# A two-layer streaming encoder step: order of the mixer's front, the bank of its first projection, and the engine of the norms' sums

## The chip, the cores and the metric

The kernel runs on one core of a Trainium2 chip. The metric is the device time of one execution in microseconds. A core has a matrix engine (TensorE, PE), a vector engine (VectorE, DVE), a scalar engine (ScalarE, ACT), GpSimd (POOL) and queues for DMA (SyncE issues nearly all of them). Each engine works through its own list of instructions in order, and waits on semaphores for the others. The matrix engine writes to PSUM, which has eight banks here; DVE and ACT read it.

## The reference

384 rows (256 prompt frames, 8 × 16 sample frames) of width 1024 pass through two layers. Each layer is

```python
x += 0.5 * rmsnorm(swiglu(rmsnorm(x)))        # ffn1
n  = rmsnorm(x); h = n @ w_in                 # mixer: one projection, split into groups
# query latent (384) | kv latent (256) | rope key (32) | conv 2x256 | gMLP 2x256 | short conv 3x256 | gates 4x1024
y  = sum_b sigmoid(gate_b) * (branch_b @ w_br_b);  x += rmsnorm(y @ w_o)
x += 0.5 * rmsnorm(swiglu(rmsnorm(x)))        # ffn2

def rmsnorm(x, g):
    return x * rsqrt(mean(x * x, -1) + EPS) * g
```

The four branches are an attention over compressed latents (the query and kv latents are each normalised, then expanded), a depthwise convolution of width 31, a gMLP with a layer norm of its right half, and a short convolution. The outputs are x and the new caches (normalised kv latents, rotated rope keys, convolution states, gMLP rows).

## The kernel before

All matrix products are made of three matmuls: each fp32 operand is split into a high part (`wh`, `xh`: copied by ACT to a rounded type) and a low part (`wl`, `xl`: the difference, by DVE), and high × high, high × low and low × high are added in PSUM. The 384 rows are three tiles of 128 (t = 0, 1, 2; t = 2 is the sample). Weights arrive by DMA in a stage (`st`), and become `wh` and `wl` shortly before use; their order is a list of units (`plan_units`, `plan_mixer`, line 565).

**Banks.** Six banks of PSUM are accumulators, `acc(t, h)`; two are used in turn as `rot`. A new tile in a bank waits for all readers of the one before it.

**Order.** The program is written by a planner. The main line of the code emits matmuls one after the other; every matmul moves an assumed clock on (`tick`). Short chains of work, such as a norm with its transposes, are generators that are spawned beside it: each `yield` names the engine that must be done first, and the chain goes on when the assumed time of that engine (costs in `COST`, line 51, and a latency) has come, in the midst of the matmuls of the main line. So costs decide between which matmuls a transpose stands; the order is then fixed on each engine, and only semaphores count on the chip.

**A passage between two stages** (`tails`, `heads`, `chain`, lines 371 to 450). The last stage's sums stand in the accumulators. For each t: ACT squares both halves with a row sum (`junk<-acc`), DVE adds the two sums and EPS in one `tensor_scalar` (`factor`), POOL raises that to the power −0.5 (`power`, tiles `post`), DVE scales and adds to x. Then the same for the next stage's norm (`pre`): square, DVE sum, POOL power, DVE product (`half`). `flip(h)` transposes each half of the normalised tile into `acc(t, h)` by four matmuls with `ident`; ACT copies the result to `xh`, and `low` lets DVE compute `xl` from the same bank. `heads` runs the next stage's first projection for t = 0, 1, 2, each of 24 matmuls (8 blocks of `xh` by `wh` and `wl`, then 8 of `xl` by `wh`).

**The mixer's front** (in layer 0 about 290 to 350 us, in layer 1 about 1210 to 1270 us). In `heads` the first projection (`main`, 416 columns: query latent and rope key, in a `rot` bank) is followed by `latent_q(t)`: ACT squares it (tile `cq`), DVE computes the rope key from it in four operations (`kr`), DVE, POOL and DVE make the norm, and its transposes go to `acc(t, 0)`. Then follow in the main line: the first half of the convolution's inputs, `conv(0)` (two projections of 24 matmuls each, in `rot`); the second projection (`mB`, 512 columns in `acc(t, 1)`), with the chains `latent_kv(t)` (tile `kv`, transposes of `half`, for t = 2 of `lat_s`) and `gmlp_v(t)` (tile `sv`); the queries (`uq`: three small projections with `rotate(t)`, whose results are transposed again, and four with `nope(j)`, which fill `qTp`); then `conv(1)`, keys, values and attention. The remaining dense work (`dense`, line 837) is put between the steps of the attention.

Of the kernel before, what the change touches and what calls it, by code (L numbers as in the profile page):

```python
# [50 lines left out]
COST = {ACT: (95, 0.83), DVE: (65, 1.04), POOL: (150, 2.1)}  # L51
# [10 lines left out]
class Engine:  # L62
# [5 lines left out]
    def __getattr__(self, op):  # L68
# [4 lines left out]
        def call(*args, **kw):  # L73
# [7 lines left out]
            else:  # L81
# [4 lines left out]
                if self.name == DVE and op == "tensor_scalar":  # L86
                    per *= 0.6
                self.core.spend(self.name, fix * (2 if "accum_out" in kw else 1) + per * n)
# [11 lines left out]
class Core:  # L100
# [224 lines left out]
    def power(self, r, v):  # L325
        self.nc.gpsimd.tensor_tensor(r, v, self.neghalf, op=ALU.pow)
# [70 lines left out]
    def chain(self, t, post, stats, gain, at=None):  # L397
# [164 lines left out]
    def plan_mixer(self, units, l):  # L562
# [7 lines left out]
        fm(range(0, 2))  # L570
        for h in range(4):
            units.append((("mB", l, h), a["in_b"][l, :, 2 * h:2 * h + 2, :], [2, 512], "M"))
        for h in range(3):
            units.append((("uq", l, h), a["w_uq"][l, h], [3, 256], "M"))
# [71 lines left out]
    def mixer_front(self, l, m, mf, ma, aT, yT):  # L646
# [201 lines left out]
        with pool("mixq") as mq:  # L848
# [11 lines left out]
            def main(t):  # L860
                pas[t] = self.rot([416])
                return pas[t], lambda k: [w[:, k % 2, :] for w in self.weights(keys[k // 2])]

            def mid(t):
                self.spawn(("cq",), latent_q(t), "rot")

            def latent_q(t):
# [4 lines left out]
                s, v, r = self.rms_stats(pa[:, :QL], "cq")  # L872
# [15 lines left out]
                self.drop("rot")  # L888
# [11 lines left out]

            def latent_kv(t, pb):
                tt = slice(t * P, (t + 1) * P)
                yield PE

                s, v, r = self.rms_stats(pb[:, :KL], "kv")
                yield ACT
                nc.vector.tensor_scalar(v, s, 1.0 / KL, EPS, op0=ALU.mult, op1=ALU.add)
                yield DVE
                self.power(r, v)
                yield POOL  # L910
                lat = lat_s if t == 2 else self.half()[:, :KL]
                nc.vector.scalar_tensor_tensor(lat, pb[:, :KL], r, g_kv, op0=ALU.mult, op1=ALU.mult)
                nc.sync.dma_start(out=a["o_lat"][l, tt, :], in_=lat)
                self.drop("acc")
                yield DVE
                tp = self.acc(t, 0)
                for j in range(2):
                    nc.tensor.transpose(tp[:, j * P:(j + 1) * P], lat[:, j * P:(j + 1) * P], self.ident)
                yield PE
                t2 = tp[:, :KL].rearrange("p (a b) -> p a b", a=2)  # L920
                if t < 2:
                    yield from self.split_into(lth[:, :, tt], ltl[:, :, tt], t2)
                else:
                    nc.scalar.copy(latTs, t2)

            def gmlp_v(t, pb):

                yield PE
                sv = self.small.tile([P, 10], F32, tag="sv", name="sv")
                nc.vector.bn_stats(sv[:, 0:6], pb[:, KL:])  # L930
                nc.vector.bn_aggr(sv[:, 6:8], sv[:, 0:6])
                v, r = sv[:, 8:9], sv[:, 9:10]
                nc.vector.tensor_scalar(v, sv[:, 7:8], EPS, None, op0=ALU.add)
                nc.vector.scalar_tensor_tensor(vn[t], pb[:, KL:], sv[:, 6:7], vn_g, op0=ALU.subtract, op1=ALU.mult)
                yield DVE
                self.power(r, v)
                yield POOL
                nc.vector.scalar_tensor_tensor(vn[t], vn[t], r, vn_b, op0=ALU.mult, op1=ALU.add)
                if t == 2:
                    nc.sync.dma_start(out=a["o_vc"][l], in_=vn[t])  # L940

            for t in range(NT):
                tt = slice(t * P, (t + 1) * P)
                pb = self.acc(t, 1)
                for k in range(KD):
                    w = self.weights(("mB", l, k // 2))
                    self.mm3(pb, (self.xh[:, k, tt], self.xl[:, k, tt]),
                             (w[0][:, k % 2, :], w[1][:, k % 2, :]), k == 0, k == KD - 1)
                    if t == NT - 1 and k % 2:
                        self.done(("mB", l, k // 2))  # L950
                self.spawn(("lat",), latent_kv(t, pb), "acc")
# [584 lines left out]
```

## Time and profile before

| | |
|---|---|
| median of 3 runs | 1859.82 us (1858.51 to 1859.93) |
| profiled execution | 1858.79 us, its span 1857.0 us |
| PE busy | 1831.8 us, 99 % |
| DVE busy | 952.6 us, 51 % |
| ACT busy | 699.7 us, 38 % |
| POOL busy | 47.7 us, 3 % |
| chain that ended last | PE 93 %, DVE 4 %, ACT 1 %, issue 1 % |

Every instruction is issued through one wrapper (line 74), so groups are told apart by their tiles, not by lines. A matmul's busy time overlaps that of the next one; the time from start to start is what it costs in a row of its like.

### The profile page before, as it was taken

Reading aid. Unit: us, or ns where it says so; the run is one execution under the profiler, and the core shown is the slowest. Engines: PE = TensorE matmul, PEld = TensorE weight load, DVE = VectorE, ACT = ScalarE, POOL = GpSimd, SP = SyncE. Lnnn points to the kernel's source line nnn. Section 1 sums busy time; section 2 is a strip of 40 time slices with the busy share of each in tenths; the row PEclk is TensorE's granted clock in tenths of the full one; section 3 lists DMA queues with packets and bytes.
Section 4 is the critical chain, followed back from the end, with each engine's and each line's share of the span. In section 5 each row is a group of like instructions: output and inputs, shape, how many; then the busy total and the mean of one; then the engine's idle time right before and its main releaser. Section 6 shows DMA issues by size and latency. Waiting matters only on the chain.

```text
span 1857.0 us, 25073 instructions
## 1 busy us (share of the span) xinstructions
PE 1831.8 (99%) x10060; PEld 1704.4 (92%) x10060; DVE 952.6 (51%) x1466; ACT 699.7 (38%) x1156; POOL 47.7 (3%) x96
## 2 busy tenths in 40 slices
PE   8999999999999999999999999999999999999998
PEld 6999998889999889999989999988899998999997
DVE  5333347896544463333463333478864446533333
ACT  5333334444333443333343333445343335333332
POOL 0000001000000000000000000010000000000000
PEclk9999999999999999999999999999999999999999
DMA  7444443452343443344444434344523434443441
GB/s 252 137 125 125 125 146 94 142 178 83 114 137 124 146 159 125 125 126 126 134 137 126 128 130 129 117 102 139 173 73 127 142 123 136 148 127 126 133 125 46
DMA packets 98087, 241.88 MB, mean 130 GB/s; under 512 B 28977, under 2 KB 39985, under 8 KB 97970
## 3 DMA queue, kind: packets, MB, share of 16 engines
q1 hardware_dynamic: 97826, 240.21, 41.4%
q8 instruction: 79, 1.29, 0.3%
q14 instruction: 38, 0.31, 0.1%
q10 hardware_dynamic: 144, 0.07, 0.0%
HBM read 236.63 MB, written 3.31 MB: 129 GB/s over the span
## 4 chain that ended last, share of the span: by engine, by line
PE 93%; DVE 4%; ACT 1%; issue 1%; POOL 0%; DMA 0%; POOLq 0%; DVEq 0%; ACTq 0%
PE rot L74 59%; PE acc L74 34%; DVE yTb L74 1%; DVE wl L74 1%; DVE half L74 1%; ACT wh L74 0%; ACT junk L74 0%; DVE sv L74 0%; DVE yTd L74 0%; DVE qTp L74 0%; DVE qa L74 0%; DVE xl L74 0%; DMA st<-in_f 0%; POOL ln L74 0%; POOL kv L74 0%
## 5 line engine op out<-in xcount | busy, mean ns | idle before, releaser
L74 DVE TENSOR_TENSOR wl<-st,wh 128x1024 fp32r<-128x1024 f32 (+3 forms) x426 | 500.1, 1185 | 479.3 <-ACT wh L74 468.3
L74 ACT CAST wh<-st 128x1024 fp32r<-128x1024 f32 (+3 forms) x426 | 428.5, 1018 | 665.1 <-issue 366.3
L74 PE MATMUL rot<-xh,wh 128*128 128x384 f32 x1984 | 669.1, 337 | 0.7 <-ACT sg L74 0.7
L74 PE MATMUL rot<-xh,wl 128*128 128x384 f32 x1984 | 665.7, 336 | 0.6 <-DVE wl L74 0.6
L74 PE MATMUL rot<-xl,wh 128*128 128x384 f32 x1984 | 665.1, 335 | 0.0
L74 PEld LDWEIGHTS rot<-xh,wh 128*128 128x128 f32 x1984 | 372.5, 188 | 8.0 <-issue 3.2
L74 PEld LDWEIGHTS rot<-xh,wl 128*128 128x128 f32 x1984 | 372.6, 188 | 5.0 <-DVE wl L74 1.0
L74 PEld LDWEIGHTS rot<-xl,wh 128*128 128x128 f32 x1984 | 372.5, 188 | 0.3 <-issue 0.3
L74 PE MATMUL acc<-wl,hh 128*128 128x512 f32 x528 | 207.2, 392 | 0.0
L74 PE MATMUL acc<-wh,hl 128*128 128x512 f32 x528 | 207.1, 392 | 0.0
L74 PE MATMUL acc<-wh,hh 128*128 128x512 f32 x528 | 205.4, 389 | 0.0
L74 DVE TENSOR_TENSOR hf<-sg,rot 128x384 f32<-128x384 f32 x80 | 44.4, 555 | 146.0 <-PE rot L74 146.0
L74 PEld LDWEIGHTS acc<-wl,hh 128*128 128x128 f32 x528 | 99.1, 188 | 20.8
L74 PEld LDWEIGHTS acc<-wh,hl 128*128 128x128 f32 x528 | 99.1, 188 | 19.1
L74 PEld LDWEIGHTS acc<-wh,hh 128*128 128x128 f32 x528 | 99.2, 188 | 18.9
L74 ACT ACTIVATE half<-rot 128x384 f32<-128x384 f32 x58 | 28.5, 492 | 167.2 <-PE rot L74 167.2
L74 DVE SCALAR_TENSOR_TENSOR half<-half,acc 128x384 f32<-128x384 f32 x44 | 24.4, 554 | 124.1 <-PE acc L74 124.1
L74 DVE SCALAR_TENSOR_TENSOR yTb<-bs,cols,yTb 128x384 f32<-128x384 f32 x120 | 73.8, 615 | 2.1
L74 PE MATMUL rot<-wl,xh 128*128 128x512 f32 (+1 forms) x144 | 55.7, 387 | 1.6 <-DVE wl L74 1.6
L74 PE MATMUL rot<-wh,xh 128*128 128x512 f32 (+1 forms) x144 | 56.3, 391 | 0.0
L74 PE MATMUL acc<-ident,half 128*128 128x128 f32 x262 | 43.9, 283 | 6.7 <-DVE half L74 5.4
L74 POOL TENSOR_TENSOR post<-post,neghalf 128x1 f32<-128x1 f32 x18 | 12.2, 679 | 1440.2 <-DVE post L74 1440.0
(221 smaller groups left out, 1631.7 us busy)
## 6 DMA issues: line engine op xcount, KB each, us to landing
st<-ffn_gp SPq DMA_DIRECT2D x160, 512.0 KB, 3.5
st<-ffn_dn SPq DMA_DIRECT2D x88, 512.0 KB, 3.5
st<-in_g SPq DMA_DIRECT2D x64, 512.0 KB, 3.7
st<-in_f SPq DMA_DIRECT2D x24, 512.0 KB, 4.0
st<-ffn_gs SPq DMA_DIRECT2D x16, 512.0 KB, 4.8
st<-w_o SPq DMA_DIRECT2D x16, 512.0 KB, 4.2
st<-w_br SPq DMA_DIRECT2D x16, 384.0 KB, 3.1
st<-in_b SPq DMA_DIRECT2D x8, 512.0 KB, 4.9
```

What stands on the lines that cost most here:

```text
L74: r = f(*args, **kw)
```

## The change

Four things are altered.

1. The first projection of the mixer goes to `acc(t, 1)` instead of a `rot` bank, and `latent_q` is a holder of an `acc` bank.
2. The queries (`uq`, with `rotate` and `nope`) stand directly behind `conv(0)`, ahead of the second projection `mB`. The order of the weights is changed with them. `latent_kv` and `gmlp_v` are moved behind them, too.
3. In `dense` the two `mix` steps follow each other, ahead of the two `short_gate` steps.
4. The sums of all norms go from DVE to POOL: one `tensor_tensor` add of EPS (for norms of two halves: EPS to the first sum early, `early`, and the second sum later), then the power. The scale 1/n of the latents' norms is folded in the Square. The planner's cost for POOL is 270 ns plus 2.1 per element instead of 150, and 330 per element for a power.

```diff
-COST = {ACT: (95, 0.83), DVE: (65, 1.04), POOL: (150, 2.1)}
+COST = {ACT: (95, 0.83), DVE: (65, 1.04), POOL: (270, 2.1)}
...
+                if self.name == POOL and kw.get("op") == ALU.pow:
+                    fix, per = 270, 330
...
-    def power(self, r, v):
+    def power(self, r, v, more):
+
+        self.nc.gpsimd.tensor_tensor(v, v, more, op=ALU.add)
         self.nc.gpsimd.tensor_tensor(r, v, self.neghalf, op=ALU.pow)
...
             squared = self.ready(ACT)
+            post.early(stats)
...
             nc.scalar.activation(self.junk(512), x[:, half(h)], AF.Square, scale=1.0 / 32, accum_out=(s0, s1)[h])
+            if h == 0:
+                yield ACT
+                nc.gpsimd.tensor_tensor(v, s0, self.eps, op=ALU.add)
         yield ACT
-        nc.vector.tensor_scalar(v, s0, s1, EPS, op0=ALU.add, op1=ALU.add)
-        yield DVE
-        self.power(r, v)
+        self.power(r, v, s1)
...
-            for f, c in ((short, 0), (short, 1), (mix, 0), (short_gate, 0), (mix, 1), (short_gate, 1), (mix_gate, 0), (mix_gate, 1),
+            for f, c in ((short, 0), (short, 1), (mix, 0), (mix, 1), (short_gate, 0), (short_gate, 1), (mix_gate, 0), (mix_gate, 1),
...
             def main(t):
-                pas[t] = self.rot([416])
+                pas[t] = self.acc(t, 1)[:, :416]
...
-                self.spawn(("cq",), latent_q(t), "rot")
+                self.spawn(("cq",), latent_q(t), "acc")
...
-                s, v, r = self.rms_stats(pa[:, :QL], "cq")
+                s, r = self.rms_stats(pa[:, :QL], "cq")
...
                 yield ACT
-                nc.vector.tensor_scalar(v, s, 1.0 / QL, EPS, op0=ALU.mult, op1=ALU.add)
-                yield DVE
-                self.power(r, v)
+                self.power(r, s, self.eps)
...
-                self.drop("rot")
+                self.drop("acc")
...
-        st = self.stat(tag, 3)
-        self.nc.scalar.activation(self.junk(elements(x)), x, AF.Square, accum_out=st[0])
+        st = self.stat(tag, 2)
+        self.nc.scalar.activation(self.junk(elements(x)), x, AF.Square, scale=elements(x) ** -0.5, accum_out=st[0])
...
+    def early(self, stats):
+        self.nc.gpsimd.tensor_tensor(stats[2], stats[0], self.core.eps4, op=ALU.add)
+
     def factor(self, stats):
         s0, s1, v, r = stats
-        self.nc.vector.tensor_scalar(v, s0, s1, EPS * self.f, op0=ALU.add, op1=ALU.add)
-        yield DVE
-        self.core.power(r, v)
+        self.core.power(r, v, s1)
```

On PE, in layer 0 at the end of the first projection of t = 0 and the start of that of t = 1, the program before had (`acc<-ident,half` are transposes of x's tile t = 1, the projection is the one with 416 columns):

```order
1462 L74 MATMUL acc<-ident,half 128x128 x3
1463 L74 MATMUL rot<-wl,xh 128x416
1464 L74 MATMUL acc<-ident,half 128x128 [waits DVE_49]
1465 L74 MATMUL acc<-ident,half 128x128 x3
1466 L74 MATMUL rot<-wh,xh 128x416
1467 L74 MATMUL rot<-wl,xh 128x416
1468 L74 MATMUL rot<-wh,xh 128x416
1469 L74 MATMUL rot<-wl,xh 128x416
1470 L74 MATMUL rot<-wh,xl 128x416 x8
1471 L74 MATMUL rot<-wh,xh 128x416 [waits Activation_49]
1472 L74 MATMUL rot<-wl,xh 128x416
```

The same place on PE in the changed program:

```order
1468 L74 MATMUL acc<-ident,half 128x128 [waits DVE_49]
1469 L74 MATMUL acc<-ident,half 128x128 x3
1470 L74 MATMUL acc<-wh,xl 128x416
1471 L74 MATMUL acc<-ident,half 128x128 [waits DVE_49]
1472 L74 MATMUL acc<-ident,half 128x128 x3
1473 L74 MATMUL acc<-wh,xl 128x416 x3
1474 L74 MATMUL acc<-wh,xh 128x416 [waits DVE_49,PE_49,Activation_49]
1475 L74 MATMUL acc<-wl,xh 128x416
```

The transposes of t = 1 have moved from twelve matmuls ahead of the projection's end to three, and the first matmul of the next projection now waits for DVE, too. The DVE instruction meant is the second `xl` of t = 1, row 158 below.

On DVE, around the same boundary, before (`x` and `post` are the residual and the norm of t = 2; `kr` is the rope key of t = 0):

```order
160 L74 TENSOR_TENSOR x_100<-x_100,half 128x512 [waits DVE_49]
161 L74 TENSOR_TENSOR xl<-acc,xh 128x4x128 [waits Activation_49] x2
162 L74 TENSOR_TENSOR kr<-rot,rope_t 128x32 [waits Activation_49]
163 L74 TENSOR_TENSOR kr<-rot,rope_t 128x16 x2
164 L74 TENSOR_TENSOR kr<-kr 128x32 [waits DVE_49]
165 L74 TENSOR_SCALAR cq<-cq 128x1
166 L74 TENSOR_SCALAR pre<-pre 128x1 [waits Activation_49]
167 L74 SCALAR_TENSOR_TENSOR half<-rot,cq,rows 128x384 [waits Pool_49]
```

And in the changed program, down to the next boundary:

```order
154 L74 TENSOR_TENSOR xl<-acc,xh 128x4x128 [waits Activation_49]
155 L74 TENSOR_TENSOR kr<-acc,rope_t 128x32 [waits Activation_49]
156 L74 TENSOR_TENSOR kr<-acc,rope_t 128x16 x2
157 L74 TENSOR_TENSOR kr<-kr 128x32 [waits DVE_49]
158 L74 TENSOR_TENSOR xl<-acc,xh 128x4x128
159 L74 SCALAR_TENSOR_TENSOR half<-acc,cq,rows 128x384 [waits Pool_49]
...
164 L74 TENSOR_TENSOR kr<-acc,rope_t 128x32 [waits Activation_49]
165 L74 TENSOR_TENSOR kr<-acc,rope_t 128x16 x2
166 L74 TENSOR_TENSOR kr<-kr 128x32 [waits DVE_49]
167 L74 TENSOR_TENSOR xl<-acc,xh 128x4x128 x2
```

The `kr` operations, which read the finished projection, stand ahead of one `xl` at the first boundary and of two at the second; the sums of `cq` and `pre` are gone from DVE.

On PE, at the transposes of `lat_s` in layer 0, before:

```order
1687 L74 MATMUL acc<-cql,wh 128x384
1688 L74 MATMUL acc<-cqh,wh 128x384 [waits PE_49]
1689 L74 MATMUL acc<-ident,lat_s 128x128 [waits DVE_49,PE_49]
1690 L74 MATMUL acc<-ident,lat_s 128x128
1691 L74 MATMUL acc<-cqh,wl 128x384
```

And after, where matmuls on `rot` with 384 columns are those of `conv(1)`:

```order
1738 L74 MATMUL rot<-xh,wh 128x384
1739 L74 MATMUL rot<-xh,wl 128x384
1740 L74 MATMUL acc<-ident,lat_s 128x128 [waits DVE_49]
1741 L74 MATMUL acc<-ident,lat_s 128x128
1742 L74 MATMUL rot<-xl,wh 128x384
```

The transposes stood among the query projections and now stand near the end of the first projection of `conv(1)`.

## Rows read from the trace of the kernel before

**Rows 1.** Page, part 1: busy us (share of the span) and instructions.

```profile
PE 1831.8 (99%) x10060; PEld 1704.4 (92%) x10060; DVE 952.6 (51%) x1466; ACT 699.7 (38%) x1156; POOL 47.7 (3%) x96
```

**Rows 2.** Waits of PE: waiter <- awaited: us in total, times, longest us.

```profile
PE acc L74 <- DVE half L74: 5.4, 8, 2.3
PE acc L74 <- DVE qTp L74: 3.1, 2, 1.6
...
PE rot L74 <- DVE wl L74: 2.3, 2, 1.6
```

**Rows 3.** Timeline, PE, first boundary: start us, us, instruction, [idle before <- releaser].

```profile
296.33 0.72 PE L74 MATMUL rot<-wh,xl 128*128 128x416 f32 x3
296.89 0.35 PE L74 MATMUL rot<-wh,xh 128*128 128x416 f32 x1
```

**Rows 4.** Timeline, ACT, at the two boundaries.

```profile
297.15 0.49 ACT L74 ACTIVATE junk<-rot 128x384 bf16<-128x384 f32 x1 [0.23 <-PE rot L74]
...
302.54 1.22 ACT L74 CAST xh<-acc 128x512 fp32r<-128x512 f32 x2 [0.34 <-PE acc L74]
303.65 0.49 ACT L74 ACTIVATE junk<-rot 128x384 bf16<-128x384 f32 x1
304.03 0.20 ACT L74 ACTIVATION_READ_ACCUMULATOR junk<-rot 128x1 f32 x1
```

**Rows 5.** Timeline, DVE, second boundary.

```profile
304.27 0.35 DVE L74 TENSOR_TENSOR kr<-rot,rope_t 128x32 f32<-128x32 f32 x3 [1.18 <-ACT junk L74]
...
304.77 1.28 DVE L74 TENSOR_TENSOR xl<-acc,xh 128x512 fp32r<-128x512 f32 x2
```

**Rows 6.** Timeline, PE, DVE and POOL, the norm of cq, t = 2.

```profile
309.30 0.35 PE L74 MATMUL rot<-wh,xl 128*128 128x416 f32 x1
...
314.48 0.41 PE L74 MATMUL rot<-xh,wh 128*128 128x384 f32 x1 [0.66 <-ACT sg L74]
...
312.06 1.22 DVE L74 TENSOR_TENSOR wl<-st,wh 128x1024 fp32r<-128x1024 f32 x1
313.72 0.62 DVE L74 SCALAR_TENSOR_TENSOR half<-rot,cq,rows 128x384 f32<-128x384 f32 x1 [0.44 <-POOL cq L74]
...
312.22 1.46 POOL L74 TENSOR_TENSOR cq<-cq,neghalf 128x1 f32<-128x1 f32 x1 [5.48 <-DVE cq L74]
```

**Rows 7.** Timeline, PE, stalls at transposes in layer 0.

```profile
307.44 0.33 PE L74 MATMUL acc<-ident,half 128*128 128x128 f32 x1 [0.60 <-DVE half L74]
...
342.94 0.30 PE L74 MATMUL acc<-ident,half 128*128 128x128 f32 x1 [0.52 <-DVE lat_s L74]
...
343.54 0.34 PE L74 MATMUL acc<-cqh,wh 128*128 128x384 f32 x1
345.44 0.45 PE L74 MATMUL acc<-ident,lat_s 128*128 128x128 f32 x1 [1.57 <-DVE qTp L74]
```

**Rows 8.** Windows: us, busy of each engine, PEclk (granted share), DMA share, GB/s.

```profile
342.00:345.40 3.40, 1.35 (x8) 0.74 (x6) 2.86 (x9) 0.75 (x2) 0.00 (x0) 0.97 0.51 177
345.40:348.40 3.00, 2.96 (x11) 2.89 (x12) 2.42 (x4) 0.79 (x3) 0.00 (x0) 0.50 0.57 164
1260.00:1264.00 4.00, 1.99 (x11) 1.40 (x9) 3.43 (x12) 1.11 (x3) 0.00 (x0) 1.00 0.49 183
1264.00:1267.00 3.00, 2.91 (x19) 2.90 (x19) 2.04 (x3) 0.80 (x3) 0.00 (x0) 1.00 0.25 53
```

**Rows 9.** Groups on POOL by form: xcount | busy us, mean ns | idle before.

```profile
L74 POOL TENSOR_TENSOR post<-post,neghalf 128x1 f32<-128x1 f32 x18 | 12.2, 679 | 1440.2 <-DVE post L74 1440.0
...
L74 POOL TENSOR_TENSOR cq<-cq,neghalf 128x1 f32<-128x1 f32 x6 | 5.1, 853 | 31.5 <-DVE cq L74 31.5
...
L74 POOL TENSOR_TENSOR sv<-sv,neghalf 128x1 f32<-128x1 f32 x6 | 3.3, 549 | 46.2 <-DVE sv L74 46.2
L74 POOL TENSOR_TENSOR ln<-ln,neghalf 128x6 f32<-128x6 f32 x2 | 2.7, 1332 | 42.3 <-DVE ln L74 42.3
```

**Rows 10.** Timeline, DVE, the last norm of the program.

```profile
1850.88 0.69 DVE L74 TENSOR_TENSOR half<-acc,gain 128x512 f32<-128x512 f32 x1 [1.86 <-ACT junk L74]
1851.48 0.20 DVE L74 TENSOR_SCALAR post<-post 128x1 f32<-128x1 f32 x1
```

More of the change, by code (lines that the diff above doesn't have):

```diff
@@ L570, in plan_mixer @@
         fm(range(0, 2))
+        for h in range(3):
+            units.append((("uq", l, h), a["w_uq"][l, h], [3, 256], "M"))
         for h in range(4):
             units.append((("mB", l, h), a["in_b"][l, :, 2 * h:2 * h + 2, :], [2, 512], "M"))
-        for h in range(3):
-            units.append((("uq", l, h), a["w_uq"][l, h], [3, 256], "M"))
         fm(range(2, 4))
@@ L899, in mixer_front @@
             run(conv(0))
[L901 to L907, printed above, removed]
-                yield DVE
[L909 to L951, printed above, removed]
-                self.spawn(("vn",), gmlp_v(t, pb), "acc")
@@ L1008, in mixer_front, with latent_kv, gmlp_v @@
                     self.done(("uq", l, 1 + j // 2))
+            def latent_kv(t, pb):
+                tt = slice(t * P, (t + 1) * P)
+                yield PE
+                s, r = self.rms_stats(pb[:, :KL], "kv")
+                yield ACT
+                self.power(r, s, self.eps)
+                yield POOL
+                lat = lat_s if t == 2 else self.half()[:, :KL]
+                nc.vector.scalar_tensor_tensor(lat, pb[:, :KL], r, g_kv, op0=ALU.mult, op1=ALU.mult)
+                nc.sync.dma_start(out=a["o_lat"][l, tt, :], in_=lat)
+                self.drop("acc")
+                yield DVE
+                tp = self.acc(t, 0)
+                for j in range(2):
+                    nc.tensor.transpose(tp[:, j * P:(j + 1) * P], lat[:, j * P:(j + 1) * P], self.ident)
+                yield PE
+                t2 = tp[:, :KL].rearrange("p (a b) -> p a b", a=2)
+                if t < 2:
+                    yield from self.split_into(lth[:, :, tt], ltl[:, :, tt], t2)
+                else:
+                    nc.scalar.copy(latTs, t2)
+            def gmlp_v(t, pb):
+                yield PE
+                sv = self.small.tile([P, 10], F32, tag="sv", name="sv")
+                nc.vector.bn_stats(sv[:, 0:6], pb[:, KL:])
+                nc.vector.bn_aggr(sv[:, 6:8], sv[:, 0:6])
+                r = sv[:, 8:9]
+                nc.vector.scalar_tensor_tensor(vn[t], pb[:, KL:], sv[:, 6:7], vn_g, op0=ALU.subtract, op1=ALU.mult)
+                yield DVE
+                self.power(r, sv[:, 7:8], self.eps)
+                yield POOL
+                nc.vector.scalar_tensor_tensor(vn[t], vn[t], r, vn_b, op0=ALU.mult, op1=ALU.add)
+                if t == 2:
+                    nc.sync.dma_start(out=a["o_vc"][l], in_=vn[t])
+            for t in range(NT):
+                tt = slice(t * P, (t + 1) * P)
+                pb = self.acc(t, 1)
+                for k in range(KD):
+                    w = self.weights(("mB", l, k // 2))
+                    self.mm3(pb, (self.xh[:, k, tt], self.xl[:, k, tt]),
+                             (w[0][:, k % 2, :], w[1][:, k % 2, :]), k == 0, k == KD - 1)
+                    if t == NT - 1 and k % 2:
+                        self.done(("mB", l, k // 2))
+                self.spawn(("lat",), latent_kv(t, pb), "acc")
+                self.spawn(("vn",), gmlp_v(t, pb), "acc")
             run(conv(1))
```

7 lines of the change are left out of this document (5 added, 2 removed).

## The prediction

> **What bounds the kernel now.** I read the shares of the engines first. TensorE (PE) is busy 99 % of the span [rows 1], so no other engine is a bound as a whole, and a change of order can only win or lose the little time in which PE stands still. The list of what PE waits for says where that is: apart from the start of the program (the longest of the waits for `half`, and the longest of those for `wl`) it names above all the transposes of normalised tiles (`half`, 5.4 − 2.3 = 3.1 us in 7 places) and `qTp` (3.1 us, 2 places) [rows 2], and with less `lat_s` and one `rot` bank. All of these lie in the front of the mixer, once in each of the two layers. So I went to the PE timeline of that stretch (about 290 to 350 us in layer 0, 1210 to 1270 us in layer 1) and measured each stall from matmul start to matmul start, less the usual pitch (0.17 us for 384 columns, 0.19 for 416, 0.23 for 512). This gives about 0.16 us more than the listed idle time: from 343.54 to 345.44 are 1.90 us, less 0.17 makes 1.73 where 1.57 are listed [rows 7].
>
> In layer 0 the stalls are: 0.76 at the cq transposes of t = 1 [rows 7]; 0.83 where the second projection of `conv(0)` waits for a `rot` bank, idle 0.66 at 314.48 [rows 6]; 0.62 and 0.39 at the latent transposes (in [rows 2], what is left of `half` is (3.1 − 2 × 0.60) / 5 = 0.38 idle in the mean); 0.69 at the rotated queries and 1.73 at `lat_s` [rows 7]. After this last gap the granted clock is 0.50, that is 1.2 instead of 2.4 GHz, for three microseconds [rows 8]: they hold 11 matmuls, most of 384 columns, which would have taken some 1.65 us at 0.15 on average (a transpose 0.11, a matmul 0.17). The slow clock has cost about 1.35 us. Sum: **6.4 us**. Layer 1 has the same places without the slow clock (granted 1.00, [rows 8]), and a wait of 0.8 for the first conv weights (`wl`, 2.3 − 1.6 = 0.7 idle in [rows 2]) in place of the bank: **5.1 us**.
>
> **The first projection in an accumulator bank.** This removes the wait for the `rot` bank, but the bank it takes instead, `acc(t, 1)`, is the one into which the second half of x of the same t has just been transposed. That bank is free when DVE has computed `xl<-acc,xh` from it. The order of the changed program shows two facts. The transposes of the next t have moved from the middle of a 24-matmul projection to its end (3 matmuls from the end for t = 1, one for t = 2), and on DVE the four `kr` operations of the finished projection now stand ahead of the `xl` that frees the bank. `kr` waits for ScalarE's Square (`junk`), which reads the finished projection, so it can't start before its last matmul. So PE's first matmul of projection t + 1 waits for a chain that begins when its last matmul of projection t ends: nothing stands between them on PE. Before, this boundary cost nothing: three matmuls from 296.33 on, the next at 296.89 [rows 3].
>
> Its price from rows. Last matmul start to Square start: the third matmul of the group at 296.33 starts at 296.33 + 2 × 0.19 = 296.70, Square at 297.15: 0.45 [rows 3, 4]. Square with its READ: 303.65 to 304.23, 0.58; READ to `kr` 0.04; the `kr` operations, from 304.27 until `xl` starts at 304.77, 0.50; one `xl`: two take 1.28, of which the second begins about 0.60 after the first, so 0.68 for the last; DVE to PE 0.14 (314.34 to 314.48) [rows 4 to 6]. Together 2.39, less the pitch of 0.19 that PE would need anyway: **2.2 us at the second projection**. At the third, Square also stands behind two `xh` copies (1.22 for two, [rows 4]) of transposes that end one matmul before: 0.4 later; and two `xl` stand behind `kr`, 0.6 more: **3.1 us**. At the first, the chain of x's t = 1 and the `xl` of t = 0 come about 0.7 us after PE is ready; I take 0.7 (0 to 1). That is 6.0 us per layer, **+12.0 us** for two. This is the firmest term: every link is a data dependence with a row of its own. Bounds 10 to 13.
>
> **What goes and what comes back.** Taking away all stalls of both layers listed above would be −6.4 − 5.1 = **−11.5 us**. But part of them returns:
> - The cq transposes of t = 2 now stand after 21 of 24 matmuls of the next projection, 21 × 0.17 + 0.19 = 3.8 us after the last one of cq's own. The chain before took 309.30 to 314.34, 5.0 us, because the power on GpSimd (312.22, 1.46 us) ended 0.40 after the `wl` of DVE beside it [rows 6]. One DVE operation less and a smaller `wl` in the new order make it some 4.4: +0.65 per layer (0 to 1.3).
> - Latent transposes (two per layer): as before, one matmul earlier, and the new norm chain is longer (below): 0.75 each (0.4 to 1.1), 1.5 per layer.
> - `lat_s`: the queries no longer hold its bank, its transposes stand after 23 matmuls of `conv(1)` and wait for its own norm: 0.35 (0 to 0.8). The 1.73 and the slow clock of layer 0 go.
> - Rotated queries: tight behind `conv(0)`, 0.2 in layer 0. In layer 1 the weights' wait of 0.81 stays, since the new order has the same copy and `wl` behind the cq transposes of t = 1.
>
> That is 2.7 in layer 0 and 3.3 in layer 1, **+6.0 us** (3 to 8.5).
>
> **Norms on GpSimd.** The removed DVE operation takes 0.20 us (1851.48, [rows 10]) and a hop to GpSimd of about 0.08 (estimated: such hops between two engines are 0.04 to 0.14 above). The added `tensor_tensor` isn't in the trace on one column: a power of one column takes 0.55, of six 1.33 [rows 9], so 0.157 per element, and 0.39 would be the fixed part; the bounds are 0.20 (what DVE takes for the sum) and 0.55 (the power). I take 0.39, the power without its work on the element, and 0.08 from one GpSimd operation to the next: each norm is longer by 0.39 + 0.08 − 0.20 = 0.27, less what the bounds of the hops leave open, I take 0.24 us, where nothing stands in its way. Most norms lie under matmuls and cost nothing; if that cover were gone, the 18 of `post` [rows 9] alone would cost 18 × 0.24 = 4.3 us. Exposed are the start (one place) and the two tightest tiles at each of three passages between stages: 7 × 0.24 = **+1.7 us** (0 to 3.5). At the very end the sum no longer stands behind DVE's product `half<-acc,gain` (0.69 us from 1850.88, while the sum came at 1851.48) [rows 10]: it is ready 0.6 earlier, and the norm is 0.24 longer: **−0.4 us**. The planner's new costs for these operations only move transposes, and that is in the places above. The two mixes side by side change two switches of matmul shape per layer: 0 ± 0.4.
>
> The trace bears on one more rule. GpSimd's power of one column took 0.55 alone and 1.46 beside `wl<-st,wh`, which reads two SBUF operands [rows 6, 9]. The Trainium skill, GPSIMD Engine Reference, section 1 Specifications, says that GpSimd shares its SBUF interfaces with VectorE and contends with instructions of two SBUF inputs; the trace agrees. By that rule each norm has two exposed operations where it had one; the sum above has no such term, and case (d) prices it from the rows.
>
> **The clock.** New gaps of 2.2 and 3.1 us are longer than the 1.57 that preceded the slow clock in layer 0; in layer 1 the same gap left it at 1.00 [rows 8]. There are four such gaps; I take one fall at the measured 1.35: **+1.4 us** (0 to 5.4). [...]
>
> **Sum.** 12.0 − 11.5 + 6.0 + 1.7 − 0.4 + 1.4 = **+9.2 us**. The profiled execution took 1858.79 us, 1.0 below the median of 1859.82. On the median this is 1869.0 us.
>
> **The rivals.** (a) *The old waits vanish and the new ones cost half* (faster). If DVE computed the bank's `xl` before `kr`, the boundary would cost only transposes, copy and `xl`, about 0.14 + 0.6 + 0.68 less the 0.2 to 0.6 of matmuls behind them, some 0.9 each: 3.6 us at four boundaries instead of 12.0. With less than half of what returns and no fall of the clock this is 3.6 − 11.5 + 2.4 + 1.3 = −4.2, 1855.6 us. With these terms the sign turns at new waits of 7.8 us in the two layers together, and the gain can be measured below 4.1. Against it stands the order of DVE, where `kr` comes first in both layers. (b) *A swap of waits*: while PE stands at the boundaries, weights and small chains catch up, so that nothing returns and no norm is exposed: 12.0 − 11.5 − 0.4 = about 0, 1860 us. For it: DVE is only half busy [rows 1] and the returning terms are my least sure ones. (c) *The clock falls after every large gap*: 4 × 1.35 = 5.4 instead of 1.4: 1873 us. For it is the fall in layer 0 after a shorter gap, against it the same gap of layer 1. (d) *GpSimd contention*: each exposed norm pays the 0.9 of 1.46 − 0.55 once more: 7 × 0.9 + 1.7 instead of 1.7, 1875 us. It needs such a `wl` at just that moment each time, and of the groups of powers in [rows 9] cq's mean, 0.85, is far above 0.55, `post` is at 0.68 and `sv` at 0.55. (e) *It doesn't do what it says*: the order shows that it does, so only the size is open.
>
> **How the numbers follow.** The forecast, +5 to +12: 0.58; (c) 0.12; (d) 0.06; (b) 0.13; (a) 0.11. What a measurement of this kernel can tell from no change is about 0.2 %, 3.7 us. The forecast, (c) and (d) are slower by more: 0.76. Faster is (a) but for a small part: 0.10. Within it are (b) and that part: 0.14. The range from 1859 to 1875 takes in the forecast, (c), most of (d) and (b)'s upper half, and leaves out some 0.2.
>
> **What would show it.** Right: in the trace of the changed kernel PE has two idle times per layer ahead of `acc<-wh,xh` with 416 columns, released by DVE `xl`, of some 2 and 3 us; the waits for `qTp` and for the `rot` bank are gone; those for `half` stay near 3 us outside the start; the time between Square's READ and GpSimd's power is 0.4 to 0.5 us. Wrong: if those two boundaries show less than 1 us, the first term falls and the time is below 1860; if GpSimd's add takes 0.1 us, the norms are shorter than before and the third term changes its sign; a granted clock of 0.50 right after the boundaries, more than once, makes it (c).

## The result

| | before | changed |
|---|---|---|
| median of 6 runs | 1858.55 us (1858.47 to 1859.93) | 1876.07 us (1872.75 to 1878.28) |
| ratio | | 1.0091, 95 % interval 1.0078 to 1.0104 |
| profiled execution, span | 1858.79, 1857.0 us | 1876.02, 1874.2 us |
| mean granted clock of PE | 0.998 | 0.995 |

The change costs 17.5 us in the medians and 17.2 us in the profiled executions. The direction was forecast, and the two main gaps at the new bank to a tenth of a microsecond; the size was not: 1869.0 us was forecast, and 1876.07 lies above the upper end of 1875.

### The profile page after: what moved, and what is told of

It is laid out like the page before. It is cut to its first block, busy times and chain, and to the rows that moved or that the text cites. A ratio compares the mean times of both kernels' runs of the same rounds, so it can differ in the third digit from the quotient of the medians.

```text
span 1874.2 us, 25145 instructions
## 1 busy us (share of the span) xinstructions
PE 1836.8 (98%) x10060; PEld 1707.1 (91%) x10060; DVE 945.9 (50%) x1414; ACT 700.5 (37%) x1156; POOL 74.6 (4%) x186
## 5 line engine op out<-in xcount | busy, mean ns | idle before, releaser
L74 POOL TENSOR_TENSOR post<-post,eps 128x1 f32<-128x1 f32 x18 | 8.8, 488 | 1419.3 <-ACT junk L74 1162.8
L74 PE MATMUL acc<-wh,xh 128*128 128x416 f32 (+1 forms) x96 | 40.5, 421 | 10.9 <-DVE xl L74 10.0
L74 PEld LDWEIGHTS acc<-ident,half 128*128 128x128 f32 x262 | 33.2, 144 | 19.1 <-DVE half L74 9.6
```

Source lines behind the costliest of these rows:

```text
L74: r = f(*args, **kw)
```

## The profile after

Waits of PE in the changed kernel (waiter <- awaited: us in total, times, longest), which answer to [rows 2]:

```profile
PE acc L74 <- DVE xl L74: 10.0, 5, 2.9
PE acc L74 <- DVE half L74: 6.0, 6, 3.2
PE acc L74 <- DVE wl L74: 3.7, 3, 1.7
```

The `xl` wait is new and the largest, that for `qTp` has gone, and there is a second new one: matmuls into an accumulator that wait for low weights. `half` without the start is 2.8 us, where it was 3.1.

The PE timeline at the boundaries to the second and the third projection, layer 0 (start, us, instruction, [idle before <- releaser]); [rows 3] is the first of the two before:

```profile
296.90 0.81 PE L74 MATMUL acc<-wh,xl 128*128 128x416 f32 x3
299.75 0.42 PE L74 MATMUL acc<-wh,xh 128*128 128x416 f32 x1 [2.04 <-DVE xl L74]
...
307.37 0.43 PE L74 MATMUL acc<-wh,xl 128*128 128x416 f32 x1
310.68 0.43 PE L74 MATMUL acc<-wh,xh 128*128 128x416 f32 x1 [2.87 <-DVE xl L74]
```

And ACT and DVE at the first of them, as [rows 4, 5]:

```profile
297.81 0.49 ACT L74 ACTIVATE junk<-acc 128x384 bf16<-128x384 f32 x1
298.20 0.19 ACT L74 ACTIVATION_READ_ACCUMULATOR junk<-acc 128x1 f32 x1
...
298.42 0.35 DVE L74 TENSOR_TENSOR kr<-acc,rope_t 128x32 f32<-128x32 f32 x3 [0.56 <-ACT junk L74]
298.81 0.19 DVE L74 TENSOR_TENSOR kr<-kr 128x32 f32<-128x32 f32 x1
298.92 0.68 DVE L74 TENSOR_TENSOR xl<-acc,xh 128x512 fp32r<-128x512 f32 x1
```

This is the chain of the prediction, link by link: Square, READ, `kr`, `xl`, and at 299.60 + 0.15 PE.

The windows behind the four gaps (us, busy and instructions of PE, PEld, DVE, ACT, POOL, then the granted clock, DMA share, GB/s):

```profile
299.60:302.60 3.00, 2.85 (x11) 2.80 (x12) 1.94 (x4) 0.35 (x2) 0.75 (x2) 0.71 0.07 14
310.60:313.60 3.00, 2.92 (x9) 2.83 (x10) 0.46 (x1) 0.00 (x0) 0.00 (x0) 0.58 0.00 0
1225.10:1228.10 3.00, 2.82 (x10) 2.72 (x11) 1.98 (x4) 0.38 (x2) 0.74 (x2) 0.62 0.04 5
1236.00:1239.00 3.00, 2.79 (x8) 2.70 (x9) 0.59 (x2) 0.00 (x0) 0.00 (x0) 0.51 0.02 5
```

All four contain a stretch at the lower level, 1.2 GHz, in which nine to ten matmuls of 416 columns each take 0.35 instead of 0.19 us: about 1.5 us lost each time. Such a stretch is called a fall of the clock below.

Where the time went, by places. Each number is the sum, over the matmuls of the place, of the time from start to start less the median of their form; a small part of each line is what a change of shape costs anyway.

| place | forecast | measured |
|---|---|---|
| new gaps at the projections (t = 0; 1; 2), both layers | +0.7; +2.2; +3.1 twice = +12.0 | +0.3; +2.2; +3.1 twice = +11.2 |
| slow clock behind them, less what stood there | +1.4 | +5.9 |
| old stalls gone, layers 0 and 1 | −11.5 | −11.5 |
| of these back: cq t = 2, latents, rotated queries, conv weights | +6.0 | +4.9 |
| waits for weights of the second projection | – | +5.3 |
| norms at the start and the passages | +1.7 | +0.5 |
| the last norm, to the end | −0.4 | −0.3 |
| rest of the mixer's front (attention, mixes) | 0 | −0.7 |
| first matmul after a stall, small shares | – | +1.9 |
| sum | +9.2 | +17.2 |

The second unforeseen line, in layer 1, is this on PE:

```profile
1267.27 0.50 PE L74 MATMUL acc<-wl,xh 128*128 128x512 f32 x1 [1.48 <-DVE wl L74]
...
1268.85 0.50 PE L74 MATMUL acc<-wh,xh 128*128 128x512 f32 x1 [0.39 <-ACT wh L74]
...
1271.25 0.50 PE L74 MATMUL acc<-wl,xh 128*128 128x512 f32 x1 [1.66 <-DVE wl L74]
```

and on ACT and DVE just ahead of it:

```profile
1258.92 0.77 ACT L74 ACTIVATE qTp<-acc 32x256 f32<-32x256 f32 x2 [1.74 <-DVE qTp L74]
1260.24 0.78 ACT L74 ACTIVATE qTp<-acc 32x256 f32<-32x256 f32 x2 [0.55 <-DVE qTp L74]
...
1267.59 0.28 ACT L74 ACTIVATE qTs<-acc 128x128 f32<-128x128 f32 x1 [1.98 <-DVE qTp L74]
1267.76 1.04 ACT L74 CAST wh<-st 128x1024 fp32r<-128x1024 f32 x1
...
1259.32 0.88 DVE L74 TENSOR_SCALAR qTp<-acc 32x256 f32<-32x256 f32 x2 [0.44 <-ACT qTp L74]
1260.65 0.89 DVE L74 TENSOR_SCALAR qTp<-acc 32x256 f32<-32x256 f32 x2 [0.44 <-ACT qTp L74]
...
1264.61 0.43 DVE L74 TENSOR_SCALAR qTp<-acc 64x256 f32<-64x256 f32 x1 [1.05 <-ACT qTp L74]
...
1266.00 1.22 DVE L74 TENSOR_TENSOR wl<-st,wh 128x1024 fp32r<-128x1024 f32 x1
1267.13 0.42 DVE L74 TENSOR_SCALAR qTp<-acc 64x256 f32<-64x256 f32 x1
1269.11 0.42 DVE L74 TENSOR_SCALAR qTp<-acc 64x256 f32<-64x256 f32 x1 [1.55 <-ACT qTp L74]
...
1269.98 1.21 DVE L74 TENSOR_TENSOR wl<-st,wh 128x1024 fp32r<-128x1024 f32 x1
```

The copies that fill `qTp` alternate between the two engines and each waits for the one before; all of them write the same tile. While an engine waits there, the copy to `wh` or the difference `wl` behind it in its queue waits, too: `wh` at 1267.76 stood behind a `qTs` copy that had waited 1.98 us for DVE, and the two `wl` that PE waits for longest, at 1266.00 and 1269.98, stood behind `qTp` copies that had waited 1.05 and 1.55 us for ACT. Between those copies and `wl` stand steps of the convolution as well (`yTb`, about 1.0 and 0.5 us), so the copies are not all that makes them late.

## The experiments

The kernel before had medians of 1859.43, 1858.62 and 1858.59 us in the three groups of four in which they ran.

**The bank taken back (e1_rot_bank).**

```diff
-                pas[t] = self.acc(t, 1)[:, :416]
+                pas[t] = self.rot([416])
```

(with `latent_q` as a holder of `rot`).

> The changed kernel with its first projection back in a rot bank, all else as changed. Theory (bank): the four idle times of 2.0 and 2.9 us ahead of the projections of t = 1 and t = 2 (9.8 us idle, 10.6 from start to start), the small ones at t = 0 (0.6) and the four stretches of half clock behind them (some 1.7 us each, 6.9) all go, 18 us; about 0.8 us per layer come back where conv(0) waits for the rot bank: 1876.1 - 18 + 1.6 = 1859.6 us. Rival (norms on GpSimd): the gaps come from late norms, so that the bank changes less than 4 us: above 1872. Rival (weights): the bank is worth 10.6 but the clock's falls have another cause: 1867.

Measured: 1860.58 us (1859.14 to 1862.02), ratio to before 1.0007 (0.9997 to 1.0016). The boundaries are closed but for 0.33 us idle at t = 2 (released by the `xh` copy), no clock falls behind them, and the wait for a rot bank in `conv(0)` does not come back (0.47 from start to start at the cq transposes of layer 0 is left there). The bank is worth 15.5 us of the 17.5; all the rest of the change together comes out even.

**The gaps filled with work of no use (e2_fill_gaps).**

```diff
+            if t and not first and len(o.shape) == 2 and o.shape[1] == 416:
+                wh, z = w(0)[0], self.rot([416])
+                for _ in range((0, 10, 15)[t]):
+                    self.tc.nc.tensor.matmul(z, lhsT=self.xh[:, 0, tt.start - P:tt.start], rhs=wh, start=True, stop=True)
             self.need(("xT", t))
```

> The changed kernel with 10 and 15 matmuls of no use (416 columns, into a free rot bank) ahead of the projections of t = 1 and t = 2, 1.9 and 2.85 us of work in gaps of 2.0 and 2.9 us. Nothing waits less. Theory (the clock's falls follow from the gaps and cost 1.7 us each): granted clock 1.00 in the four stretches behind, 1876.1 - 6.9 = 1869 us, and the runs no longer spread from 1872.8 to 1878.3. Rival (the time behind the gaps is lost to something other than the clock, weights or late chains): 1876 or more.

Measured: 1866.83 us, and four runs within 0.3 us. Two of the four windows behind the gaps:

```profile
299.60:302.60 3.00, 2.85 (x16) 2.83 (x16) 1.97 (x4) 0.38 (x2) 0.74 (x2) 1.00 0.06 13
311.00:314.00 3.00, 3.00 (x18) 2.57 (x17) 0.85 (x2) 0.80 (x2) 0.00 (x0) 1.00 0.00 0
```

The clock stays at 2.4 GHz in all four, and the changed kernel is 9.2 us faster by fifty matmuls whose results nobody reads. Of this 1.6 are not the clock: in layer 1 the waits for the second projection's weights are 1.3 us here instead of 4.0, with the rotated queries and the latent transposes waiting 1.2 more. Of the rest most is the clock: four falls of about 1.5 us, some 6 us where 6.9 were expected. The spread of the changed kernel fits this, too: its run at 1872.75 had a mean clock of 0.997, that at 1878.28 one of 0.994. A mean lower by 0.003 over 1874 us is some 11 us more at half the clock, by estimate three falls of ten matmuls at 0.35 us, or 5 us; the two runs lie 5.5 apart.

**The rope key issued behind the power (e3_key_behind).** The four `kr` operations and their DMA stand behind `self.power(r, s, self.eps)`:

```diff
                 s, r = self.rms_stats(pa[:, :QL], "cq")
                 kr = self.small.tile([P, 3, RD], F32, tag="kr", name="kr", bufs=2)
...
-                nc.vector.tensor_tensor(kro, kr[:, 0, :], kr[:, 1, :], op=ALU.add)
                 yield ACT
                 self.power(r, s, self.eps)
+                nc.vector.tensor_tensor(kro, kr[:, 0, :], kr[:, 1, :], op=ALU.add)
```

> The changed kernel with the four rope key operations issued behind the power of the cq norm instead of ahead of it, so that on DVE both xl stand ahead of them; the bank stays an accumulator. Theory (DVE order): the gap at t = 1 is transposes, copy and xl only, 1.0 us instead of 2.2, at t = 2 1.4 instead of 3.1; the clock does not fall: 1876.1 - 2 x 2.9 - 6.9 = 1863.4 us. If the clock still falls twice, 1867. Rival (bank as such costs, whatever DVE does first): 1874 or more.

Measured: 1866.72 us (1864.83 to 1867.36). The gaps are 1.00 and 1.45 us from start to start in both layers, as expected, with a granted clock of 1.00 behind all four. The median is 3.3 above the 1863.4 expected. The profiled execution, 1864.83, is the fastest of the four, and 1.4 above what was expected: in its layer 0 the first matmul of the second projection waits 1.17 us for a rotated query (`qr`), which it did not do in the changed kernel. The other three runs are 2 us longer, at mean clocks of 0.997 to 0.998 against 0.999; by the same estimate that is one or two falls each, but where they stand no trace shows. Which operation frees the bank, and behind what it stands, is worth some 9 us.

**The queries back behind the second projection (e4_queries_behind).** The block of `rotate`, `nope` and their loops, and their weights in `plan_mixer`, stand behind `mB`:

```diff
         fm(range(0, 2))
-        for h in range(3):
-            units.append((("uq", l, h), a["w_uq"][l, h], [3, 256], "M"))
         for h in range(4):
             units.append((("mB", l, h), a["in_b"][l, :, 2 * h:2 * h + 2, :], [2, 512], "M"))
+        for h in range(3):
+            units.append((("uq", l, h), a["w_uq"][l, h], [3, 256], "M"))
```

> The changed kernel with the queries and their weights behind the second projection again, as before; bank, sums and mixes as changed. Theory (the second projection's weights come too late behind the short queries): the waits for wh and wl of 1.3 us in layer 0 and 4.0 in layer 1 and the 0.8 at the rotated queries go, and the old waits at the rotated queries and at lat_s return (2.4 and 2.5 us, with or without one fall of the clock of 1.4): 1875 to 1876.5 us. Rival (the weights are late because of the GpSimd sums or the bank): those waits stay and the old ones come in addition, 1880.

Measured: 1876.77 us (1875.13 to 1877.87). The time is the one expected, but not by the sum expected. The waits for weights go, all 5.3 us, yet ahead of `lat_s` PE now waits longer than it ever did:

```profile
PE acc L74 <- DVE qTp L74: 7.9, 2, 4.0
```

Behind both of these waits, 3.96 us idle each, the clock fell as well, which the expected sum had at most once. So the move of the queries exchanges one victim for another: either `lat_s`, whose bank is held by a query, or the weights of the second projection.

**The alternating copies (e5_one_engine_queries).** All else as changed:

```diff
-                    if i % 2:
-                        nc.vector.tensor_scalar(y, x, SM_SCALE, None, op0=ALU.mult)
-                    else:
-                        nc.scalar.mul(y, x, SM_SCALE)
+                    nc.scalar.mul(y, x, SM_SCALE)
...
-                nc.scalar.mul(qTp[0:64, 2 * j, :], o[0:64, :TP], SM_SCALE)
+                nc.vector.tensor_scalar(qTp[0:64, 2 * j, :], o[0:64, :TP], SM_SCALE, None, op0=ALU.mult)
```

> The changed kernel, but the copies of the rotated queries into qTp all on ScalarE and those of the seven other query results into qTp all on VectorE, where they alternated. Theory (the second projection's weights come late because the two engines that make wh and wl wait for each other at every alternating copy, some 0.44 us each): most of the waits for wh and wl behind the queries (1.3 us in layer 0, 4.0 in layer 1) and of the 0.8 and 0.3 at the queries go; gaps and clock at the bank stay: 1876.1 - 5 = 1871 us. Rival (the weights are late by DMA or by space in the ring): those waits stay within 1 us, 1875 to 1876.5.

Measured: 1867.61 us (1865.37 to 1869.48), 8.5 below the changed kernel. On ACT the rotated queries now go through in one piece:

```profile
1252.05 3.08 ACT L74 ACTIVATE qTp<-acc 32x256 f32<-32x256 f32 x8 [2.37 <-PE acc L74]
...
1261.08 0.28 ACT L74 ACTIVATE qTs<-acc 128x128 f32<-128x128 f32 x1 [1.74 <-DVE qTp L74]
1261.26 1.04 ACT L74 CAST wh<-st 128x1024 fp32r<-128x1024 f32 x1
```

The waits for the second projection's weights fall from 5.3 to 2.8 us, that of 0.8 at the queries is gone, and the latent transposes of t = 0 in layer 0 wait 0.62 instead of 1.28. 2.8 us of weights remain. The second line shows that part of this is the copies still: a `qTs` copy on ACT waits 1.74 us for DVE's `qTp`, and `wh` stands behind it. What is left without any such wait no run shows. Three of the 9.3 us between the two profiled executions are the clock and not the copies: in this one the clock stayed up behind the two gaps of 2.04 us, while it fell behind those of 2.87 (here layer 0, where both gaps lie ahead of the first copy):

```profile
299.90:302.90 3.00, 3.00 (x16) 2.98 (x17) 1.78 (x3) 0.18 (x2) 0.74 (x2) 1.00 0.06 14
309.20:312.20 3.00, 2.94 (x10) 2.85 (x11) 0.44 (x1) 0.00 (x0) 0.00 (x0) 0.58 0.00 0
```

**Both (e6_rot_one_engine).** The edits of e1_rot_bank and e5_one_engine_queries together.

> Both: first projection in a rot bank as in e1_rot_bank (1860.6), and qTp's copies of one kind on one engine. Theory: 1860.6 - 5 = 1855.6 us, faster than the kernel before. Rival (weights late by DMA or ring): 1860 to 1861.

Measured: 1853.28 us (1852.91 to 1856.25), ratio 0.9974 (0.9964 to 0.9984): with the bank given back and the copies in order, the rest of the change is 5.3 us faster than the kernel before. Against e1_rot_bank the copies give 7.3 us here where 5 were expected. The runs below show that the gain over the kernel before is the copies alone.

**The sums alone (e7_sums_alone).** Of the diff, only `power`, `early`, `factor`, `rms_stats` and the planner's costs.

> The kernel before with the norms' sums on GpSimd and the planner's new costs alone; bank, queries and mixes as before. From e4_queries_behind (1876.8) without its bank (10.6 + 0.6 of waits, 6.9 of slow clock) and with the wait for the rot bank back (1.6): 1860.3 us; the waits for qTp ahead of lat_s are near 4 us in each layer instead of 1.6, and others shorter. Rival (the sums are what makes the change slow): above 1866. Rival (they gain, and the rest loses): below 1857.

Measured: 1858.98 us (1858.13 to 1861.12), ratio 1.0000 (0.9990 to 1.0009). Moving 54 sums to GpSimd makes no difference that can be measured. In the trace it moves waits about: 4.2 instead of 1.7 us ahead of `lat_s` in each layer, 0.46 and nothing instead of 0.69 and 0.74 at the rotated queries, none at the first cq transposes, and less in the late front; the clock falls behind `lat_s` in both layers instead of one.

**The bank alone (e8_bank_alone).** Of the diff, only `pas[t] = self.acc(t, 1)[:, :416]` and its holder.

> The kernel before with the first projection in the accumulator bank alone. In its order the transposes of t = 1 stay in the middle of the projection and only at the third projection kr stands ahead of both xl. Theory (DVE's order makes the gap, the bank only lets it through): no gap at t = 1, one of 2.9 us at t = 2 with one fall of the clock (1.7) behind it, in each layer; 0.8 at the rot bank goes in layer 0: 1859.4 + 2 x (3.1 + 1.7) - 0.8 = 1868.2 us. Rival (the bank costs the full 18 us wherever it is used): 1876.

Measured: 1868.34 us (1865.40 to 1869.94), the time expected, in part by luck, with one link wrong: the gap at t = 1 is not zero. PE waits there 1.37 us for `xl`, which DVE computes ahead of `kr` but behind its work for the residual of t = 2; the clock stays up behind it, while it falls behind both gaps of 2.87 us at t = 2:

```profile
298.50:301.50 3.00, 2.95 (x16) 2.92 (x17) 2.42 (x9) 0.11 (x2) 1.06 (x2) 1.00 0.24 77
...
1231.60:1234.60 3.00, 2.98 (x9) 2.87 (x10) 0.62 (x1) 0.00 (x0) 0.55 (x1) 0.50 0.02 5
```

The two gaps at t = 1 add 3.1 us that were not expected; the profiled execution, with a mean clock of 0.996, is the slowest of the four, and the others, at 0.997 to 0.999, had fewer falls by that measure. So the bank costs 9.7 us in the order of before, and 15.5 in the order that the other parts of the change make.

**The copies alone (e9_before_one_engine).** The kernel before with the edit of e5_one_engine_queries and nothing else.

> The kernel before with nothing but the copies into qTp of one kind on one engine. Theory (the old waits ahead of lat_s are the alternating copies, too, which hold the bank that lat_s needs): the 1.7 us in each layer and the slow clock of 1.35 behind them in layer 0 go, some 0.5 stays for lat_s's own norm: 1858.6 - 4 = 1854.6 us. Rival (the bank is late because the queries come late, not because of the copies): 1858 to 1859.

Measured: 1853.54 us (1853.31 to 1853.68), ratio 0.9968 (0.9957 to 0.9980). Where PE waited 1.57 us for `qTp` [rows 7], it goes on at once:

```profile
342.84 0.41 PE L74 MATMUL acc<-ident,half 128*128 128x128 f32 x2 [0.52 <-DVE lat_s L74]
...
343.44 0.34 PE L74 MATMUL acc<-cqh,wh 128*128 128x384 f32 x1
343.62 0.38 PE L74 MATMUL acc<-ident,lat_s 128*128 128x128 f32 x2
```

and the slow clock behind it is gone. In the kernel before, the rows of ACT and DVE show what the wait was made of:

```profile
341.39 0.37 ACT L74 ACTIVATE qTp<-acc 32x256 f32<-32x256 f32 x1 [2.16 <-PE acc L74]
344.46 0.77 ACT L74 ACTIVATE qTp<-acc 32x256 f32<-32x256 f32 x2 [2.69 <-DVE qTp L74]
...
343.55 0.42 DVE L74 TENSOR_TENSOR half<-half 128x256 f32<-128x256 f32 x1
344.00 0.42 DVE L74 TENSOR_SCALAR qTp<-acc 32x256 f32<-32x256 f32 x1
344.87 0.43 DVE L74 TENSOR_SCALAR qTp<-acc 32x256 f32<-32x256 f32 x1 [0.44 <-ACT qTp L74]
```

ACT's second copy waits 2.69 us for DVE's first, and that stands on DVE behind the rope products of the other tiles (the last ends at 343.97). Only then do the turns of 0.44 us follow. So the wait that the change tried to avoid by its new order was made by the share of the copies that DVE had. The edit takes those copies off DVE and ends the alternation at once; no run separates the two.

**The planner's old costs (e10_old_costs).** The changed kernel with

```diff
-COST = {ACT: (95, 0.83), DVE: (65, 1.04), POOL: (270, 2.1)}
+COST = {ACT: (95, 0.83), DVE: (65, 1.04), POOL: (150, 2.1)}
...
-                if self.name == POOL and kw.get("op") == ALU.pow:
-                    fix, per = 270, 330
```

> The changed kernel with the planner's old cost for GpSimd (150 ns, no price for a power): the same operations on the same engines, another order. The transposes of t = 1 and t = 2 then stand in the middle of the projections, and xl ahead of kr on DVE. Theory (the raised costs put kr ahead of xl and so made the gap): no 2.9 us ahead of t = 2 and at most the 1.4 of e8_bank_alone ahead of t = 1, 1 to 2 us per layer at the transposes instead, since they now come ahead of their norms; no fall of the clock: 1876.1 - 18.1 + 2 x 1.5 + 2 x 1.5 = 1864 us. Rival (the sums on GpSimd themselves make xl late): above 1872.

Measured: 1868.04 us (1867.24 to 1870.71), between theory and rival. With the same operations, the boundary at t = 2 has no gap and that at t = 1 a small one:

```profile
297.74 1.29 PE L74 MATMUL acc<-wh,xl 128*128 128x416 f32 x6
299.55 0.46 PE L74 MATMUL acc<-wh,xh 128*128 128x416 f32 x1 [0.53 <-DVE xl L74]
```

In exchange the transposes stand ahead of their norms again: waits of 0.6 to 0.7 us from start to start for `half`, four of them at t = 1 and t = 2 of the two layers and others at the passages between the other stages, 15 in all and 9.2 us with the start.

```profile
PE acc L74 <- DVE half L74: 9.2, 15, 1.9
```

The 8 us between this and the changed kernel, in whose traces there are one and four falls of the clock, are the net price of the order that the raised costs make, with `kr` ahead of `xl`; it is a matter of costs in the planner and not of the engine of the sums. The waits for the second projection's weights in layer 1 stay at 4.0, and behind them stands a fall of the clock that was not expected.

**Sums on DVE, queries first, copies in order (e11_dve_sums_one_engine).** The kernel before with the queries ahead of `mB` and the edit of e5_one_engine_queries.

> The kernel before with the queries ahead of the second projection and the copies into qTp of one kind on one engine; sums on VectorE, rot bank, mixes as before. If the sums on GpSimd are worth nothing here (e7_sums_alone: 1859.0 against 1858.6), this is as e6_rot_one_engine, 1853.3 within 1.5 us. Rival (they help where the queries come first): 1856 or more.

Measured: 1853.39 us (1853.26 to 1854.04), ratio 0.9970 (0.9959 to 0.9982).

**Sums on GpSimd, queries behind, copies in order (e12_sums_one_engine).** As e7_sums_alone with that edit.

> As e7_sums_alone (1859.0: sums on GpSimd, queries behind the second projection, rot bank), with the copies into qTp of one kind on one engine. Its waits for qTp ahead of lat_s were 4.0 us in each layer: theory (alternating copies), 1859.0 - 2 x 3.7 = 1851.6 us, without the order of queries that the change made. Rival (the wait is for the queries, not for the copies): 1857 or more.

Measured: 1854.05 us (1853.68 to 1855.43), ratio 0.9973 (0.9961 to 0.9985), less than expected: `lat_s` still waits 1.44 us for its bank in each layer, since the four copies of the query that holds it, now in one piece on ACT, take 1.53 us and end at 342.45 in layer 0, and PE goes on at 342.51. With the copies in order, all four arrangements (e6, e9, e11, e12) lie between 1853.3 and 1854.1. Neither the order of queries nor the engine of the sums makes a measurable difference among them (of the four only e6 has the two mixes side by side, which no run changed alone), and the shortest edit, e9, is as good as any.

## Why the prediction was right or wrong

**What bounds the kernel** held: all that moved is in the front of the mixers. Outside of it the two traces agree within 0.1 us per stage, but for the start (+0.5) and the end.

**The bank** (first term, +12.0) held: 2.20 and 3.11 us from start to start in both layers where 2.2 and 3.1 were forecast, and every link within 0.1 us of its price from [rows 3 to 6] (2.2, 0.4 and 0.6 are 3.2, not the 3.1 of the prediction). Only the first projection waits less, 0.3 instead of 0.7. e1 shows that the bank is the cause, e3 that it is what stands ahead of `xl` on DVE.

**The clock** (+1.4) is the first step that failed. The mechanism was named, and its price, 1.35 from [rows 8], was near the 1.5 measured; what was wrong is the number of falls. One was taken for four gaps, after one fall and none behind two equal gaps before, though the new gaps are longer than both. There were four falls, and the term is 5.9. Case (c) had them, at 4 × 1.35 and a chance of 0.12; with it, the forecast would have been 1873. That the falls follow from the gaps e2 shows: with matmuls in the gaps the granted clock is 1.00 behind all four.

**What comes back** (+6.0) is right in the lines it has (4.9, nearly all of it the latent transposes 3.1, cq of t = 2 0.4, conv weights 0.5 and the queries 0.8; `lat_s` nothing) and lacks one: the waits for the second projection's weights, 5.3 us. This is the second step that failed: a term put at nothing, without a reason. The prediction followed what the moved queries release (`lat_s`) and not what they push: their copies stand on ACT and DVE ahead of the making of `wh` and `wl`, and those weights are now needed sooner after the copies than before. The row that could have told it was there: in [rows 7] PE waits 1.57 us with `qTp` as the releaser, and this was read as a bank that the queries hold, without asking why their copies end so late. ACT's copies wait there for DVE's, which stand behind other work; e9 removes the wait by the edit of the copies alone, and e5 by the same edit about half of the weights' waits. What makes the other half late stays open in part: e2 has 2.8 us less of them in layer 1 with the copies as they were. Either failed step alone would have left the time within the range (1869.0 + 4.5 or + 5.3); together they carried it out, and the terms that came out smaller did not make up for them.

**The norms** (+1.7) were mis-sized: the added sum takes 0.19 us and not 0.39 where nothing is in its way, about what it took on DVE (mean ns in the last column but one):

```profile
L74 POOL TENSOR_TENSOR cq<-cq,eps 128x1 f32<-128x1 f32 x6 | 1.1, 191 | 42.8 <-ACT junk L74 42.8
...
L74 POOL TENSOR_TENSOR cq<-cq,neghalf 128x1 f32<-128x1 f32 x6 | 3.3, 551 | 0.5
...
L74 POOL TENSOR_TENSOR sv<-sv,neghalf 128x1 f32<-128x1 f32 x6 | 5.4, 903 | 0.5
```

The fixed part of a power was taken for that of any operation. The passages cost nothing, the start 0.5; the contention that [rows 6] showed has moved from `cq`, 0.85 before and 0.55 now, to `sv`, 0.55 before and 0.90 now: at t = 2 of both layers its power takes 1.60 us beside a `wl<-st,wh`, the other four 0.55. Case (d) did not come. The end came as forecast: DVE's last products start 1.69 us after ACT's Square there, before 2.28, and the span is 0.3 shorter behind the last matmul.

**That the planner's costs only move transposes** was said, and falls short: with them `kr` comes ahead of `xl` on DVE. The prediction took that order as given and priced it inside the bank's term. e10 shows that near half of the loss, 8 of 17.5 us, hangs on it.

**The rivals.** (a) put the boundary with `xl` ahead of `kr` at 0.9 each; e3 has 1.00 and 1.45. It was right to hold it unlikely. (b), in which waits merely swap, is what e1 shows for all of the change but the bank. It had 0.13 for the whole, and the boundary, which did cost what was forecast, rules it out there.

## What to carry to other kernels

Before a result moves to another bank, find the instruction that frees that bank and read what stands ahead of it in its engine's order: if anything there reads the result of the matmul group that has just ended, the matmul engine stops at each boundary, however free the bank looks. Price a fall of the clock at every new gap that is as long as one behind which the trace shows it, and where a gap can't be closed, work of no use in it can pay (here about 6 us). When a wait names a tile that two engines fill in turns, look first whether one waits for the other and what stands ahead of that one in its queue, before moving the work around it. And ask of work that is moved not only what it releases, but what it now stands ahead of.

## What was not expected of the hardware

- The clock after the longer gaps of PE: after idle times of 0.84 to 1.37 us at the boundaries it was 1.00 in all six (e3, e8); after 1.44 to 1.57 us at `lat_s` it fell in one of five (1.57 in the kernel before; not in its other layer, e8 and e12), after 1.92 us in e8's other layer it fell. At the boundaries after 2.04 us it fell in three of six (both in the changed kernel, one of two in e4, none of two in e5), after 2.87 us in eight of eight (the changed kernel, e4, e5, e8); after 3.96 us at `lat_s` in four of four (e4, e7). The length of one gap does not decide alone: behind the pair of waits of 1.48 and 1.66 us for the second projection's weights it fell in e10 and stayed up in the changed kernel, e1 and e3, and in e6 it fell behind waits of 0.98 and 0.53 us.
- A fall cost about 1.5 us; two in e4 and one in e8 lasted twice as long as the others. By the mean clocks on record (0.994 to 0.997) the changed kernel has a different number of falls from run to run, which would be most of its spread of 5.5 us.
- A one-column add on GpSimd takes 0.19 us, a power of one column 0.55, where nothing is in their way.
- A stall costs some 0.16 us more from start to start than its listed idle time, and the matmul behind it up to 0.11 us more than its like (512 columns; 0.03 to 0.06 for a transpose).
